# Cumsum-difference matmul on one core: x rows come in another order among the first w blocks, copies are shared anew, and the first five groups get a new order

## The chip, the cores and the metric

The kernel runs on one NeuronCore of a Trainium2 chip. Five engines matter here: TensorE (PE) for matmuls, VectorE (DVE) and ScalarE (ACT) for elementwise work, GpSimd (POOL) for one reduction across partitions, and SyncE (SP), from which all DMA transfers are issued. The metric is the device time of one execution in microseconds; the median of three runs stands for a kernel.

## The reference

```python
def reference(x, w):
    cs = np.cumsum(x, axis=1)
    diff = cs - np.concatenate([np.zeros((cs.shape[0], 1, cs.shape[2])), cs[:, :-1, :]], axis=1)
    return np.matmul(diff, w).astype(np.float32)
```

x is (8, 2048, 2048) and w is (2048, 2048), both float32. The difference of a running sum is x again, so what is computed is x @ w: 16384 rows by 2048 by 2048. The kernel computes that product.

## The kernel before

**Tiling.** x has 128 tiles of 128 rows. The first four tiles ("plain rows") are multiplied in bf16 as they are; the other 124 in f16, in 31 groups of four tiles, by a Strassen-Winograd scheme: seven products of blocks instead of eight, and in most products a second level inside (class `Quarters`: seven quarter products; class `Whole`: eight ordinary half products). The names of the steps are those of the scheme: B11, B21, B12, B22 are scaled f16 blocks of w, T1 to T4 their sums, S1 to S4 sums of x blocks (g and h are the two row pairs of a group), P1 to P5 the five products with a second level, Q1 to Q4 and make1 to make4 the inner sums of w, s1 to s4 the inner sums of x.

**Start.** w comes as 32 blocks `w.h.k` of 128 x 1024 (column half h, row block k), 0.5 MB each. The x rows of the first four tiles come as 16 pieces `first x.q.r` (column quarter q, tile r) of 0.25 MB. DVE casts a pair of pieces (`cast x.q.a`, a = tile pair), PE transposes it through PSUM against an identity built by the `eye` steps (`turn x.q.a`), and DVE or ACT copies it back (`turned x.q.a`). A w block is cast to bf16 (`cast w.h.k`, a ring of seven buffers) and DVE finds its largest magnitude (`max w.h.k`). `plain.h.r.k` are the products of the first four tiles. Before the first of them PE runs dummies (`warm.i`), which read a tile of zeros.

**Scale.** The largest of all maxima goes over the partitions on POOL (`max of all`); from it come `uw` and `uinv`, and with `uinv` the raw w is turned into the blocks (`B11.k` and so on, line 460 on DVE, 462 on ACT). The leftover part of tile 3 (`left over.i`) uses these scaled blocks too. A later row tile t is loaded, weighed (mean magnitude, line 140, ACT), given a scale (line 163, DVE), narrowed to f16 (line 178, ACT) and transposed by DMA (`turn`, line 195).

**Groups.** Period 0 holds the plain rows and the first group, in which nearly all is done at one level. Periods 1 to 30 are one group each: products P1, P2, P5, P3, P4 with 28 matmuls each and 16 half products, 204 matmuls of 512 columns (208 in period 1, whose P1 is a `Whole`). The results leave PSUM by `keep` (a scaled copy, line 624, ACT) and by adds such as `C12g+P3.g` (line 635, DVE); `P.first` and `P.out` (line 627, ACT) copy between PSUM banks or to a chain buffer, `P.middle` and `P.last` (line 576, DVE) add to banks. All matmuls of the groups are lines 588 (half products) and 610 (quarter products).

**Order.** Each step is recorded with a label, an engine and a function; nothing is issued until the end. `emit` then sorts all steps by a key, period number times 1620 plus the label's place in the table `places`, and issues them in that order, each engine's instructions chained so that the order holds. The table has own entries for periods 0, 1, 2, 29, 30 and 31, and one (None) for all others, so period 3 uses the common one. On each engine and on SP's queue the steps run strictly in this order; between engines semaphores make a step wait for what it reads or overwrites. These are the lines that do it:

```python
        for _, _, engine, ask in sorted(ops, key=when) if places else ops:
            after(engine, ask)
```

## Time and profile before

| | before |
|---|---|
| median of 3 runs | 1450.01 us (1449.58 to 1451.32) |
| profiled execution, its span | 1449.2 us |
| PE, DVE, ACT busy | 99%, 92%, 83% of the span |
| granted PE clock, mean | 0.999 |
| DMA | 351.59 MB, mean 243 GB/s |
| first real product (`plain.0.1.0`) | 13.19 us |
| first scaled block of w | 61.04 us |
| first product of periods 2, 3, 4, 5 | 166.09, 210.98, 255.01, 299.04 us |

Times in the profile are microseconds from the span's start. A row of a timeline gives start, duration, engine, line, operation, what it writes and reads (names without buffer numbers), and in brackets how long the engine was idle before it and what ended the wait. A row of a stretch gives for each engine the busy time and the number of instructions. A row of a group gives busy time, mean duration in nanoseconds, and the idle time ahead of its instructions. A busy engine shows overlapping durations: back to back, matmuls of 512 columns start 0.216 us apart though each lasts 0.38.

### The profile page before, as it was taken

How to read it: one execution, taken by the hardware profiler on the slowest of the kernel's cores; microseconds unless marked ns; L12 is line 12 of the kernel's file. 1: busy time of each engine (PE TensorE's matmuls, PEld its weight loads, DVE VectorE, ACT ScalarE, POOL GpSimd, SP SyncE). 2: the span in 40 equal slices, each digit the busy share in tenths (PEclk: the TensorE clock that was granted, in tenths of full speed). 3: DMA queues.
4: the chain of work that ended last, by engine and by line, in shares of the span. 5: the costliest groups of instructions: out<-in, count | busy, mean ns of one | idle time of the engine just before them, and what ended most of it. 6: DMA issues, size and time to landing. Idle time of an engine off the chain costs nothing.

```text
span 1449.2 us, 20358 instructions
## 1 busy us (share of the span) xinstructions
PE 1438.6 (99%) x6692; PEld 652.2 (45%) x6698; DVE 1334.3 (92%) x2345; ACT 1204.5 (83%) x1994; POOL 0.5 (0%) x5
## 2 busy tenths in 40 slices
PE   8999999999999999999999999999999999999998
PEld 4444444444444444444444444444444444444443
DVE  6999999999999999999999999999999999999988
ACT  5997888898888888888988888988888888889783
POOL 0000000000000000000000000000000000000000
PEclk9999999999999999999999999999999999999999
DMA  9999979899888999989998888998989998989973
GB/s 360 369 252 272 252 212 228 240 247 262 226 234 226 243 262 231 244 222 228 247 265 233 228 229 237 252 257 226 222 239 244 260 248 225 218 236 248 264 200 116
DMA packets 343930, 351.59 MB, mean 243 GB/s; under 512 B 270992, under 2 KB 270992, under 8 KB 343824
## 3 DMA queue, kind: packets, MB, share of 16 engines
q1 hardware_dynamic: 343824, 350.29, 89.4%
q8 instruction: 52, 0.85, 0.2%
q14 instruction: 54, 0.44, 0.1%
HBM read 150.99 MB, written 134.22 MB: 197 GB/s over the span
## 4 chain that ended last, share of the span: by engine, by line
PE 91%; issue 4%; DMA 2%; ACT 2%; DVE 1%; DVEq 0%; POOLq 0%; ACTq 0%; SPq 0%
PE b L610 61%; PE b L588 30%; DMA x<-F 1%; DMA F<-in_x_dram 1%; DVE W L460 1%; ACT waste L140 0%; DMA out_dram<-arena 0%; ACT W L462 0%; DVE arena L635 0%; ACT arena L624 0%; ACT F L178 0%; ACT arena L342 0%; ACT arena L178 0%; DVE arena L576 0%; DVE W L576 0%
## 5 line engine op out<-in xcount | busy, mean ns | idle before, releaser
L588 PE MATMUL b<-W,x 128*128 128x512 f16 x2144 | 518.1, 379 | 0.1
L635 DVE SCALAR_TENSOR_TENSOR arena<-b,tiny,arena 128x512 f32<-128x512 f32 x612 | 446.9, 745 | 16.0 <-PE b L610 4.8
L610 PEld LDWEIGHTS <-arena 128*128 128x128 f16 x2744 | 268.2, 98 | 325.4 <-DVE arena L576 6.3
L610 PE MATMUL b<-W,arena 128*128 128x512 f16 x1672 | 413.7, 379 | 0.8 <-DVE arena L576 0.4
L624 ACT ACTIVATE arena<-b,tiny 128x512 f32<-128x512 f32 x496 | 317.0, 684 | 35.4 <-PE b L588 14.9
L588 PEld LDWEIGHTS <-x 128*128 128x128 f16 x2144 | 209.7, 98 | 253.3 <-issue 0.3
L140 ACT ACTIVATE waste<-F,tiny 128x1024 uint8<-128x1024 f32 x246 | 283.9, 1154 | 15.6 <-DMA F<-in_x_dram 14.1
L178 ACT ACTIVATE F<-F,tiny 128x1024 f16<-128x1024 f32 x246 | 282.1, 1147 | 10.9 <-DVE tiny L163 9.4
L610 PE MATMUL b<-W,x 128*128 128x512 f16 x1192 | 287.5, 379 | 0.0
L610 PE MATMUL b<-arena 128*128 128x512 f16 x1072 | 261.6, 379 | 0.0
L610 PEld LDWEIGHTS <-x 128*128 128x128 f16 x1428 | 139.7, 98 | 168.5
L576 DVE TENSOR_TENSOR b<-b,arena 128x512 f32<-128x512 f32 x298 | 205.9, 691 | 5.7 <-ACT arena L627 2.0
L627 ACT COPY b<-b 128x512 f32<-128x512 f32 x149 | 85.5, 574 | 134.4 <-PE b L610 112.4
L627 ACT COPY arena<-b 128x512 f32<-128x512 f32 x298 | 170.2, 580 | 19.9 <-PE b L610 13.0
L576 DVE TENSOR_TENSOR arena<-W 128x2048 f16<-128x2048 f16 (+1 forms) x158 | 185.6, 1176 | 0.4 <-PE b L610 0.4
L576 DVE TENSOR_TENSOR arena<-x,x 128x512 f16<-128x512 f16 (+1 forms) x181 | 91.5, 506 | 50.1 <-PE b L610 50.1
L576 DVE TENSOR_TENSOR x<-x,x 128x1024 f16<-128x1024 f16 x124 | 85.2, 687 | 2.0
L576 DVE TENSOR_TENSOR arena<-W,arena 128x512 f16<-128x512 f16 (+1 forms) x157 | 85.9, 563 | 0.6 <-PE b L610 0.5
L576 DVE TENSOR_TENSOR arena<-arena 128x512 f16<-128x512 f16 x120 | 50.8, 424 | 13.7 <-PE b L610 11.8
L610 PE MATMUL b<-arena,x 128*128 128x512 f16 x236 | 60.3, 379 | 0.0
L324 PE MATMUL b<-arena 128*128 128x512 bf16 x234 | 53.5, 379 | 1.5 <-DVE arena L279 0.8
L576 DVE TENSOR_TENSOR arena<-x,arena 128x512 f16<-128x512 f16 x119 | 49.6, 417 | 0.6 <-PE b L610 0.6
(49 smaller groups left out, 503.6 us busy)
## 6 DMA issues: line engine op xcount, KB each, us to landing
F<-in_x_dram SPq DMA_DIRECT2D x246, 512.0 KB, 5.4
out_dram<-arena SPq DMA_DIRECT2D x240, 512.0 KB, 4.8
W<-in_w_dram SPq DMA_DIRECT2D x31, 512.0 KB, 9.5
out_dram<-arena SPq DMA_DIRECT2D x31, 256.0 KB, 2.7
W<-in_x_dram SPq DMA_DIRECT2D x16, 256.0 KB, 6.6
x<-F SPq DMA_TRANSPOSE x246, 4.4
arena<-in_x_dram SPq DMA_DIRECT2D x2, 512.0 KB, 5.1
W<-in_w_dram SPq DMA_DIRECT2D x2, 256.0 KB, 9.0
```

The costliest lines, as they stand in the source:

```text
L140: lambda: nc.scalar.activation(waste, data, ABS, bias=least, scale=1.0 / ROW, accum_out=m),
L178: lambda: nc.scalar.activation(to, data, COPY, scale=s),
L324: said = nc.tensor.matmul(to[n], xP[:, r, ko, :], b[:, ds(n * NB, NB)], start=(ko == 0), stop=(ko == KO - 1),)
L460: ask = lambda: nc.vector.tensor_scalar(to, src, uinv, None, MUL)
L576: record(label, "dve", lambda: nc.vector.tensor_tensor(dst, p, q, op))
L588: said = nc.tensor.matmul(to[n], a[k], b[k][:, n, :], start=(start and k == 0), stop=(k == KH - 1), skip_group_check=True,)
L610: said = nc.tensor.matmul(to, a[k], b[k], start=(start and k == 0), stop=(k == 3), skip_group_check=True)
L624: record(label, "act", lambda: nc.scalar.activation(c, p, COPY, scale=u))
L627: record(label, "act", lambda: nc.scalar.copy(to, p))
L635: label, "dve", lambda: nc.vector.scalar_tensor_tensor(c, p, u, c, MUL, ADD)
```

## The change

Nothing is added to or removed from the computation except six dummies. Four things change.

- `WARM` falls from 30 to 24. Before, 22 dummies ran ahead of the first transpose, seven between the first and second, one more after it; in the new order 22, one and one.
- `on_two` gives each copy in two forms, for ACT and for DVE, and `record` swaps the engine of the labels in `moved`. Period 0: seven w casts (w.0.0, 0.1, 0.4, 0.7, 0.11, 1.1, 1.14), `turned x.3.1` and `B22.5` go from ACT to DVE; `cast x.2.1`, `out.0.1.0`, `out.0.2.0` and `B22.6` from DVE to ACT. Period 2: two narrows, three keeps and `P4.first` from ACT to DVE. Period 3: one narrow, three keeps and `P5.out4` from ACT to DVE.
- `places` has new orders for periods 0, 1 and 2 and an own one for period 3. On SP's queue w.0.0 comes after six x pieces instead of eight, w.0.2 and w.0.1 before the last two pieces of the second quarter; `load1.0` comes ahead of `turn0.0`. On DVE the zeros that the dummies read come after the first eye rows, and the last two eye rows after casts of x. On PE all leftover products come before the first group's.
- `plainly` and `made` replace `all_seven` and `more`: a table says which product is taken as `Whole`, and which inner sums have been made. With the table as it stands (P1 of period 1 alone) the same products and sums are issued as before.

```diff
-    WARM = 30
+    WARM = 24
...
+    moved = {
+        0: (
+            "cast w.0.0", "cast w.0.1", "cast w.0.4", "cast x.2.1", "cast w.0.7",
+            "turned x.3.1", "cast w.0.11", "cast w.1.1", "out.0.1.0", "out.0.2.0",
+            "cast w.1.14", "B22.5", "B22.6",
+        ),
+        2: (
+            "narrow4.1", "keep C12h.1", "narrow6.1", "P4.first", "keep C21g.0", "keep C21g.1",
+        ),
+        3: (
+            "narrow4.1", "keep C12g.0", "P5.out4", "keep C21g.1", "keep C21h.1",
+        ),
+    }
+
     def record(label, engine, ask):
...
+        if isinstance(ask, dict):
+            if label in moved.get(period[0], ()):
+                engine = {"act": "dve", "dve": "act"}[engine]
+            ask = ask[engine]
         ops.append((period[0], label, engine, ask))
+
+    def on_two(to, src, scale=None):
+        if scale is None:
+            return {
+                "act": lambda: nc.scalar.copy(to, src),
+                "dve": lambda: nc.vector.tensor_copy(to, src),
+            }
+        return {
+            "act": lambda: nc.scalar.activation(to, src, COPY, scale=scale),
+            "dve": lambda: nc.vector.tensor_scalar(to, src, scale, None, MUL),
+        }
+
...
-        record(
-            f"narrow{role(t)}.{i}",
-            "act",
-            lambda: nc.scalar.activation(to, data, COPY, scale=s),
-        )
+        record(f"narrow{role(t)}.{i}", "act", on_two(to, data, s))
...
     places = {
         0: {
-            'first x.0.2': 0, 'first x.1.1': 1, 'first x.0.0': 2, 'first x.1.3': 3,
-            'first x.0.3': 4, 'first x.0.1': 5, 'first x.1.2': 6, 'first x.1.0': 7, 'w.0.0': 8,
-            'zeros': 9, 'least': 10, 'ones': 11, 'numbers': 12, 'numbers turned': 13, 'eye': 14,
-            'eye#2': 15, 'eye#3': 16, 'eye#4': 17, 'cast x.0.1': 18, 'cast w.0.0': 19, 'warm.0': 20,
-            'warm.1': 21, 'warm.2': 22, 'warm.3': 23, 'warm.4': 24, 'warm.5': 25, 'warm.6': 26,
-            'warm.7': 27, 'warm.8': 28, 'warm.9': 29, 'warm.10': 30, 'warm.11': 31, 'warm.12': 32,
-            'warm.13': 33, 'warm.14': 34, 'warm.15': 35, 'warm.16': 36, 'warm.17': 37,
-            'warm.18': 38, 'warm.19': 39, 'warm.20': 40, 'warm.21': 41, 'turn x.0.1': 42,
-            'warm.22': 43, 'warm.23': 44, 'warm.24': 45, 'warm.25': 46, 'warm.26': 47,
-            'warm.27': 48, 'warm.28': 49, 'turned x.0.1': 50, 'cast x.1.0': 51, 'cast x.0.0': 52,
...
+            'ones': 1, 'first x.0.0': 1, 'least': 2, 'first x.0.2': 2, 'numbers': 3,
+            'first x.0.3': 3, 'numbers turned': 4, 'first x.1.1': 4, 'eye': 5, 'first x.0.1': 5,
+            'zeros': 6, 'first x.1.0': 6, 'eye#2': 7, 'warm.0': 7, 'w.0.0': 7, 'warm.1': 8,
+            'w.0.2': 8, 'cast x.0.1': 8, 'warm.2': 9, 'w.0.1': 9, 'eye#3': 9, 'cast w.0.2': 9,
+            'warm.3': 10, 'first x.1.3': 10, 'cast x.0.0': 10, 'warm.4': 11, 'w.0.3': 11,
+            'eye#4': 11, 'warm.5': 12, 'first x.1.2': 12, 'cast x.1.0': 12, 'warm.6': 13,
+            'w.0.4': 13, 'cast w.0.0': 13, 'warm.7': 14, 'w.0.5': 14, 'warm.8': 15,
+            'first x.2.0': 15, 'warm.9': 16, 'first x.2.2': 16, 'warm.10': 17, 'first x.2.1': 17,
+            'warm.11': 18, 'w.0.6': 18, 'warm.12': 19, 'w.0.7': 19, 'warm.13': 20,
+            'first x.2.3': 20, 'warm.14': 21, 'w.0.8': 21, 'warm.15': 22, 'first x.3.0': 22,
+            'warm.16': 23, 'w.0.9': 23, 'warm.17': 24, 'first x.3.1': 24, 'warm.18': 25,
+            'w.0.10': 25, 'warm.19': 26, 'first x.3.2': 26, 'warm.20': 27, 'first x.3.3': 27,
+            'warm.21': 28, 'w.0.11': 28, 'turn x.0.1': 29, 'w.0.12': 29, 'warm.22': 30,
+            'w.0.13': 30, 'turn x.0.0': 31, 'w.0.14': 31, 'warm.23': 32, 'w.0.15': 32,
+            'turned x.0.0': 33, 'w.1.0': 33, 'turned x.0.1': 34, 'plain.0.1.0': 34,
+            'plain.0.0.0': 35, 'cast w.0.1': 35, 'plain.0.2.0': 36, 'max w.0.2': 36,
...
+            'plain.0.3.11': 89, 'w.1.3': 89, 'turned x.3.1': 89, 'plain.0.0.11': 90,
+            'max w.0.11': 90, 'w.1.6': 90, 'plain.0.2.11': 91, 'max w.0.12': 91, 'w.1.15.0': 91,
+            'plain.0.1.11': 92, 'max w.0.14': 92, 'w.1.5': 92, 'plain.0.1.12': 93, 'max w.0.13': 93,
+            'w.1.11': 93, 'plain.0.3.12': 94, 'max w.1.0': 94, 'w.1.7': 94, 'plain.0.2.12': 95,
+            'cast w.1.1': 95, 'w.1.9': 95, 'plain.0.0.12': 96, 'max w.0.15': 96, 'w.1.8': 96,
+            'plain.0.2.13': 97, 'max w.1.4': 97, 'w.1.10': 97, 'plain.0.1.13': 98, 'max w.1.2': 98,
...
+            'plain.1.1.7': 139, 'plain.1.2.7': 140, 'plain.1.1.8': 141, 'cast w.1.14': 141,
...
+            'weigh0.0': 149, 'plain.1.3.9': 150, 'weigh0.1': 150, 'plain.1.1.10': 151, 'mean0': 151,
+            'plain.1.1.11': 152, 'unit0': 152, 'scale0': 152, 'plain.1.0.12': 153, 'B22.0': 153,
+            'B11.2': 153, 'plain.1.1.12': 154, 'B11.6': 154, 'weigh2.0': 154, 'plain.1.0.13': 155,
+            'B11.7': 155, 'narrow0.0': 155, 'plain.1.0.14': 156, 'B11.3': 156, 'narrow0.1': 156,
+            'plain.1.3.10': 157, 'B11.5': 157, 'weigh2.1': 157, 'plain.1.0.15': 158, 'B21.2': 158,
+            'plain.1.2.10': 159, 'load1.0': 159, 'B21.7': 159, 'plain.1.3.11': 160, 'turn0.0': 160,
+            'B21.0': 160, 'plain.1.3.12': 161, 'turn0.1': 161, 'B21.3': 161, 'plain.1.3.13': 162,
+            'B21.5': 162, 'plain.1.1.13': 163, 'B21.4': 163, 'plain.1.2.11': 164,
...
+            'left over.0': 173, 'out.1.3.1': 173, 'left over.1': 174, 'mean2': 174,
+            'out.1.0.0': 175, 'scale2': 175, 'left over.2': 175, 'B11.0': 176, 'weigh1.0': 176,
+            'left over.3': 176, 'T1.3': 177, 'A11g B11.0.0': 177, 'narrow2.0': 177, 'B11.4': 178,
+            'A12g B21.1.0': 178, 'out.1.3.0': 178, 'turn2.0': 178, 'T1.6': 179, 'A11g B11.0.1': 179,
...
         1: {
+            'weigh4.1': -1329, 'P1h.1.1': -1329, 'S3g': -1328, 'P5.0': -1328, 'keep C11h.0': -1328,
+            'P2.6': -1327, 'keep C11h.1': -1327, 'P5.s1': -1326, 'C11g+P2.g.1': -1325, 'S2g': -1324,
+            'put0.0': -1324, 'in1.make1.1': -1323, 'S2g T2.0.0': -1323, 'P5.1': -1322,
+            'P5.s2': -1321, 'P2.last': -1320, 'C11h+P2.h.0': -1319, 'S3h': -1318, 'P5.first': -1318,
+            'in5.make4.0': -1317, 'weigh6.0': -1317, 'P5.2': -1317, 'S2h': -1316,
+            'S2g T2.0.1': -1316, 'mean4': -1316, 'C11h+P2.h.1': -1315, 'P5.out2': -1315,
...
         2: {
+            'P3.3': -2826, 'P3.out2': -2826, 'P3.s3': -2825, 'weigh5.0': -2825, 'in3.Q3': -2824,
+            'P3.s4': -2823, 'P3.4': -2823, 'P3.middle': -2822, 'turn4.1': -2822,
+            'C12g+P3.g.0': -2821, 'P3.5': -2821, 'P3.out4': -2821, 'in4.Q1': -2820,
...
+            'mean5': -2819, 'C12h+P3.h.0': -2818, 'P4.1': -2818, 'put0.1': -2818, 'scale5': -2817,
...
+        3: {
+            'P1.0': -4420, 'P1.1': -4419, 'P2.0': -4418, 'P1.first': -4416, 'P2.1': -4415,
...
+            'keep C21h.1': 2559, 'put3.1': 2559, 'P2.s2': 2560, 'load8.1': 2560,
```

More of the change, by code (lines that the diff above doesn't have):

```diff
@@ L335, with result @@
     results_at = iter(results * 2)
-    def result(name, p, rows, columns, u=None):
+    def result(name, p, rows, columns):
         c = next(results_at)
-        if u is None and name in ("out.0.1.0", "out.0.2.0"):
-            record(f"{name}", "dve", lambda: nc.vector.tensor_copy(c, p))
-        elif u is None:
-            record(f"{name}", "act", lambda: nc.scalar.copy(c, p))
-        else:
-            record(f"{name}", "act", lambda: nc.scalar.activation(c, p, COPY, scale=u))
+        record(name, "dve" if name in ("out.0.1.0", "out.0.2.0") else "act", on_two(c, p))
         done.append(
@@ L815, in slot, with plainly, made @@
                 matmuls(*halves_of(f"{self.name}{name}", to, a, self.right, True)[at % 4])
+    def plainly(name, g):
+        return name in {PLAIN + 4: ('P1',)}.get(g, ())
+    making = {}
+    def made(name, inner, how):
+        if name not in making:
+            making[name] = True
+            how(inner)
     def group_plain(g):
@@ L972, in group @@
         P1.slot(1)
-        if more:
+        if not P1.plain:
             in_1.give("Q4")
@@ L1015, in group @@
         P1.slot(6)
-        if not more:
-            make_5(in_5)
-        in_5.give("Q3")
+        if not P5.plain:
+            made("P5", in_5, make_5)
+            in_5.give("Q3")
         C11h = keep("keep C11h", Y, uh, free.pop(1))
@@ L1033, in group @@
         total("S4g", S4g, A12g, S2g, SUB)
-        if not more:
-            make_1(in_1)
+        if not plainly("P1", g + 4):
+            made("P1", in_1, make_1)
+        if not plainly("P2", g + 4):
+            made("P2", in_2, make_2)
         go(2)
@@ L1162, in group @@
         P4.slot(6)
+        if P4.plain and not plainly("P4", g + 4):
+            made("P4", in_4, make_3)
+        if P5.plain and not plainly("P5", g + 4):
+            made("P5", in_5, make_5)
+        if P3.plain and not plainly("P3", g + 4):
+            made("P3", in_3, make_3)
         turn(next_l, [1])
```

69 lines of the change are left out of this document (38 added, 31 removed), and 454 rows, old and new, of the table places.

## The prediction

> **What bounds the kernel now.** I read the page's first part, then the table by stretches of time, then the timelines where that table shows idle time.
>
> ```profile
> PE 1438.6 (99%) x6692; PEld 652.2 (45%) x6698; DVE 1334.3 (92%) x2345; ACT 1204.5 (83%) x1994; POOL 0.5 (0%) x5
> ```
>
> TensorE (PE) is busy for 99% of the span, so little can be won. Where it isn't busy is seen by stretches; the cuts are the first real product (13.19), the scale of w (61.04), and the first product of each group from the second on.
>
> ```profile
> core 0: us, PE busy (x) PEld busy (x) DVE busy (x) ACT busy (x) POOL busy (x), PEclk, DMA share, GB/s
> 13.19:33.34 20.15, 19.88 (x111) 9.77 (x115) 14.05 (x14) 15.57 (x17) 0.00 (x0) 1.00 1.03 404
> 33.34:61.04 27.70, 27.26 (x131) 12.56 (x132) 26.82 (x28) 24.35 (x29) 0.35 (x1) 1.00 1.03 407
> 61.04:117.43 56.39, 56.04 (x258) 25.06 (x258) 55.73 (x97) 50.79 (x79) 0.00 (x0) 1.00 1.00 266
> 117.43:166.09 48.66, 47.82 (x221) 21.45 (x220) 47.05 (x103) 37.73 (x63) 0.00 (x0) 1.00 0.96 236
> 166.09:210.98 44.89, 44.89 (x209) 20.30 (x208) 43.05 (x78) 38.41 (x65) 0.00 (x0) 1.00 0.85 234
> 210.98:255.01 44.03, 44.03 (x205) 19.94 (x204) 40.93 (x73) 38.35 (x65) 0.00 (x0) 1.00 0.93 247
> 255.01:299.04 44.03, 44.03 (x205) 19.94 (x204) 40.75 (x73) 37.48 (x64) 0.00 (x0) 1.00 0.87 236
> ```
>
> From 166 us on TensorE has no idle time at all; periods 3 and 4 take 44.03 us each, and the orders from period 4 on are not touched. What can move is what lies before 166 us: the 13.19 us ahead of the first real product, and PE idle of 0.27, 0.44, 0.35 and 0.84 us in the four stretches behind it. VectorE (DVE) is nearly full there too: idle 0.88, 0.66, 1.61, 1.84 and 3.10 us in the stretches from 33.34 to 255.01. DMA is full until 61 us (share 1.03, 404 to 407 GB/s). So there are three bounds in a row: DMA, then DVE and PE together, then PE alone.
>
> The profiled execution spans 1449.2 us; the median of three runs is 1450.0, 0.8 more. I sum differences and set them against the median. What this measurement can tell from no change is about 0.2%, 2.9 us.
>
> **Start: earlier, and worth nothing.**
>
> ```profile
> 0.00:14.00 14.00, 10.31 (x57) 4.88 (x59) 7.04 (x16) 3.71 (x4) 0.19 (x4) 1.00 0.83 291
> 1.17 6.24 PE L362 MATMUL b<-arena 128*128 128x512 bf16 x22 [1.17 <-DVE arena L237]
> 9.09 0.62 PE L269 MATMUL b<-waste,W 128*128 128x128 bf16 x8 [1.68 <-DVE W L260]
> 8.34 0.69 DVE L260 CAST W<-W 128x1024 bf16<-128x1024 f32 x1 [5.08 <-DMA W<-in_x_dram]
> 11.57 1.05 ACT L313 CAST arena<-W 128x1024 bf16<-128x1024 f32 x1 [9.57 <-DMA W<-in_w_dram]
> 13.19 1.04 PE L324 MATMUL b<-arena 128*128 128x512 bf16 x3 [0.79 <-DVE arena L279]
> 33.43 7.17 DVE L305 TENSOR_REDUCE tiny<-W 128x1 f32<-128x1024 f32 x6 [0.35 <-DMA W<-in_w_dram]
> ```
>
> Today w.0.0 is the ninth transfer on SP's queue and lands at 11.57. The new order puts it seventh, two x pieces of 0.26 MB sooner: 0.52 MB at 404 GB/s is 1.3 us, so about 10.3. Its cast moves from ACT (1.05) to DVE (0.69), and "turned x.0.0" queues behind it on DVE for another 0.69: first product at about 11.7, 1.5 us sooner. "zeros" comes later on DVE, so the dummies begin about 1.2 us later; 22 of them still take 6.24 us and end by about 8.7, ahead of the second x cast and the last "eye" rows that the transposes wait for (their x lands as late as today). The six dummies left out stood in waiting time: 0.
>
> None of the 1.5 us survives. At 33.43 DVE, idle, waits for w.0.12 itself, and PE has been fed block by block until then (idle 0.27 us in 20.15). All 16 x pieces and w.0.0 to w.0.10 stand ahead of w.0.11 in both orders, and the bytes are the same. An earlier start only puts waits between 12 and 33 us. Value 0; ends -1.5 (if kept) and +0.5 (a cast on DVE stuck behind a reduction).
>
> **From w.0.11 to the scale of w.** B11 and B21 need the largest |w|, so the last reduction counts.
>
> ```profile
> 56.69 2.96 ACT L313 CAST arena<-W 128x1024 bf16<-128x1024 f32 x3 [0.31 <-DMA W<-in_w_dram]
> 49.06 10.81 DVE L305 TENSOR_REDUCE tiny<-W 128x1 f32<-128x1024 f32 x10
> 60.58 0.15 DVE L453 TENSOR_SCALAR tiny<-tiny 128x1 f32<-128x1 f32 x1 [0.48 <-POOL tiny L451]
> 61.04 2.74 DVE L460 TENSOR_SCALAR W<-W,tiny 128x1024 f16<-128x1024 f32 x4
> ```
>
> Nine whole reductions and a half one in 10.81 us: 1.13 each, 0.6 for the half. At 56.69 ACT waits for w.1.13; one block of 0.52 MB at 407 GB/s later, at about 58.0, w.1.14 is there, yet DVE's last reduction ends at 59.9: DVE is behind by 0.8. In the new order DVE has, from w.0.11's landing (one block before 33.4, so 32.1): its cast, 0.69, then 21 whole reductions (23.7), two halves (1.2), "turned x.3.1" and "cast w.1.1" (0.65 each, in place of the two copies out.0.1.0 and out.0.2.0 that go to ACT), in all to about 59.0, and w.1.14's own landing plus 1.13 allows 59.1. So 0.8 sooner. "cast w.1.14" now lies in the 0.48 us in which DVE waits for POOL; 0.1 of it sticks out. The scaled blocks begin at 60.3 instead of 61.04: **-0.7**, ends -0.9 and 0.
>
> **Blocks and first products.**
>
> ```profile
> 70.15 2.75 PE L588 MATMUL b<-W,x 128*128 128x512 f16 x12
> 75.33 10.52 PE L588 MATMUL b<-W,x 128*128 128x512 f16 x48
> L460 DVE TENSOR_SCALAR W<-W,tiny 128x1024 f16<-128x1024 f32 x18 | 12.2, 748 | 0.1
> ```
>
> Four blocks in 2.74 us (the last shows its full 0.75) are 0.66 apart. Today B22.7 is among them and the leftovers are strewn between products; at 75.33 all 11 leftover matmuls and the 16 of "A11g B11" are done. The new order makes 15 blocks in a row before the first T1, 9.9 us, with two tiny scales to 70.4; PE does all leftovers first and begins A11g at about 70.6. 16 matmuls at 0.216 (48 in 10.52) bring it to the same point at 74.1: 1.3 sooner, of which 0.7 was counted. **-0.6** more, ends -0.8 and 0.
>
> This needs row 4 transposed by 70.6. The new order puts load1.0 ahead of turn0 on SP's queue.
>
> ```profile
> 65.06 1.34 SPq L195 DMA_TRANSPOSE x<-F  x1
> 66.51 0.99 SPq L517 DMA_DIRECT2D arena<-in_x_dram  x2
> x<-F SPq DMA_TRANSPOSE x246, 4.4
> ```
>
> Issue stays near 65.5 (it hangs on load0's landing, ACT's weighing and narrowing); 4.4 us to landing gives 69.9, margin 0.7. 0; ends 0 and +1.3 (one more block of 0.52 MB ahead of it).
>
> **Waits in periods 0 and 1.** The second fence groups DVE's instructions from 61 to 255 us by form (mean in ns); back to back they start 0.08 us closer than they last.
>
> ```profile
> 86.10 3.63 PE L588 MATMUL b<-W,arena 128*128 128x512 f16 x16 [0.25 <-DVE arena L576]
> 136.99 1.02 PE L610 MATMUL b<-W,arena 128*128 128x512 f16 x4 [0.40 <-ACT b L627]
> 138.45 1.90 PE L610 MATMUL b<-W,arena 128*128 128x512 f16 x8 [0.44 <-DVE arena L576]
> 135.53 0.75 DVE L635 SCALAR_TENSOR_TENSOR arena<-b,tiny,arena 128x512 f32<-128x512 f32 x1 [0.41 <-ACT arena L624]
> ```
> ```profile
> L635 DVE SCALAR_TENSOR_TENSOR arena<-b,tiny,arena 128x512 f32<-128x512 f32 x69 | 49.7, 742 | 0.9 <-ACT arena L624 0.4 <-PE b L610 0.3
> L543 DVE SCALAR_TENSOR_TENSOR W<-W,tiny 128x1024 f16<-128x1024 f32 x8 | 9.9, 1276 | 0.0
> L576 DVE TENSOR_TENSOR W<-W 128x512 f16<-128x512 f16 x44 | 17.2, 417 | 0.1
> L576 DVE TENSOR_TENSOR x<-x,x 128x1024 f16<-128x1024 f16 x16 | 11.0, 685 | 0.2
> L576 DVE TENSOR_TENSOR arena<-W 128x2048 f16<-128x2048 f16 x15 | 18.3, 1217 | 0.2 <-PE b L610 0.2
> ```
>
> These three waits make up most of the 0.35 + 0.84 us of idle PE in the third and fourth stretches. The first is S1g: in the new DVE order eight T1 (9.5), a block, "out" and two C11g adds (0.66 each), one T2 and S1g (0.6 each), one make1 (0.33) and a scale follow on 70.4: S1g ends near 84.2, and PE arrives at 74.1 + 48 x 0.216 = 84.4. The other two come from "C11h+P2.h.0", which waits for ACT's "keep C11h.0" and holds up P5.first. The new order keeps C11h directly behind C11g, ahead of weigh6 and mean4, and puts two units of PE work between P5.0 and P5.1. **-1.2**, ends -1.5 and 0.
>
> **Eleven copies more on DVE in periods 2 and 3.**
>
> ```profile
> L340 DVE COPY arena<-b 128x512 f32<-128x512 f32 x2 | 1.4, 680 | 0.0
> L178 ACT ACTIVATE F<-F,tiny 128x1024 f16<-128x1024 f32 x37 | 42.5, 1148 | 4.2 <-DVE tiny L163 3.7
> L624 ACT ACTIVATE arena<-b,tiny 128x512 f32<-128x512 f32 x64 | 41.3, 683 | 7.4 <-DMA out_dram<-arena 3.6 <-PE b L588 3.2 <-PE b L610 0.4
> 237.95 0.42 DVE L576 TENSOR_TENSOR arena<-x,x 128x512 f16<-128x512 f16 x1 [1.88 <-PE b L610]
> ```
>
> Three narrows leave ACT (1.15 each) for DVE at a block's price, 0.66; eight copies out of PSUM (0.68 on ACT) for DVE at about 0.6 to 0.68, as L340: 2.0 + 4.9 = 6.9 us. ACT is idle 6.5 and 5.7 us in those periods, so its relief brings nothing. DVE's idle time from 61 to 255 is 7.2 us; PE coming 2.5 us earlier (0.7 + 0.6 + 1.2) takes 2.5 off. DVE begins 0.7 earlier, and the new order lets "C22h+Y.1", "keep C21h.1" and P2.s2, 1.6 us, slip behind the first product of period 4. 7.2 - 2.5 + 0.7 + 1.6 = 7.0 against 6.9: it fits only if DVE never waits. It will; 1.88 us of today's idle time is one wait for PE. Both orders added up show where: from the first block to P3.middle of period 2 DVE has 102 short sums (0.33), 63 of 0.6 to 0.65, 39 scaled adds (0.66), 20 blocks and narrows (0.66), 8 T1, 9 wide sums (1.13), 14 scales and one keep, in all 133 us, and ends at 193.6; PE, 142 units of 0.863 after 70.6, wants it at 193.2. So DVE is late by 0.4 there, and as the result is only there 0.1 to 0.2 after the next start, by some 0.6; the same for P3.4 (in3.Q3) and P4.1 (C12g+P3.g.1). I take **+0.7**, ends 0 and +4.9 (all idle time of periods 2 and 3 stays, 1.84 + 3.10). The other moves (B22.5 against B22.6, cast x.2.1) swap equals: 0.
>
> **Sum:** -0.7 - 0.6 - 1.2 + 0.7 = -1.8: **1448.2 us**, 0.12% down.
>
> **A cold clock.** Today's 22 dummies take 6.24 us, and at 0.216 apart they would take 4.9: a start of PE from rest costs 1.3. The granted clock reads 1.00 throughout, so it is the row that shows it. In the new order only two dummies, not eight, stand between the first transpose and the first product. If PE slowed down again there, it would cost at most 1.3 once more, at 12 to 16 us, where the 1.5 us that w.0.12 takes back would cover it: the sum stays at -1.8, and without that cover it is -0.5. [...]
>
> **Rivals.**
> 1. *Full gain.* DVE is never late and the waits before 61 us (0.27 + 0.44) go in part as well: -2.5 - 0.5, 1447.0. For it: every cut is where a wait stands today. Against: DVE's balance of 0.1 us.
> 2. *No gain.* w.1.14 lands where it does, and DVE meets its casts or blocks late by a reduction (1.13) or so in 32 to 60 us; P5 and period 2 get new waits for those removed: 1450.0. For it: DVE idle of 0.88 us in 27.70.
> 3. *Slower.* DVE cannot shed its waits in periods 2 and 3, so the 6.9 us come on top: +4.9 and up to 6.9 against -2.5, about 1453.5. It costs more than it brings from 2.5 us of kept idle time, and is slower by over 0.2% from 5.4. Against: DVE also waits less when PE waits.
> 4. *turn0 late*: +1.3, 1449.5.
> 5. *A second cold start, uncovered*: +1.3, 1449.5. Against: today PE idles 1.68 us before 9.09, and the stretch behind 13.19 shows 0.27 us of idle PE.
>
> **How the numbers follow.** Forecast (1447.2 to 1449.3) 0.42, full gain 0.22, no gain 0.17, slower 0.14, turn0 0.03, clock 0.02. Faster by over 0.2% is below 1447.1: rival 1, 0.22. Slower is rival 3, 0.14. The rest 0.64. The range 1446.8 to 1452.2 takes in the forecast, rivals 2, 4 and 5 and nearly all of 1, and leaves out most of 3. The likeliest case alone: 1447.2 to 1449.3.
>
> **What would show it.** First product near 11.7, yet w.0.12's reduction still near 33.4; blocks begin at 60.2 to 60.5; "A11g B11" at 70.5 to 70.8; period 2's first product about 2.5 us sooner with one unit more of period 1 behind it (near 162.7); period 4's near 253.2, then 44.03 a period; DVE idle in periods 2 and 3 down to some 2 us. I am wrong if blocks begin after 60.8, if A11g waits for a transpose, or if PE idles over 2 us between 166 and 255.

## The result: 9 us slower, made in four periods

| | before | after |
|---|---|---|
| median | 1450.25 us (1449.58 to 1451.32) | 1459.48 us (1459.07 to 1460.81) |
| ratio, 95% interval | | 1.0065 (1.0053 to 1.0078) |
| span of the profiled execution | 1449.2 us | 1457.9 us |
| first product of periods 1, 2 | 117.43, 166.09 us | 113.02, 165.81 us |
| first product of periods 3, 4, 5 | 210.98, 255.01, 299.04 us | 214.22, 262.55, 307.40 us |

(Period 1's first product comes earlier among the products of period 0 in the new order, and one unit of 0.86 us of period 1 now lies behind period 2's first product; so only the later marks compare directly.) From period 5 on the kernels need 44.03 and 44.05 us a period. Nearly all is lost before.

The page's first part and the stretches of the changed kernel, cut at the same events as before (first real product, 61.04, first product of periods 1 to 5; the cut of period 3 lies one matmul behind its first):

```profile
PE 1439.6 (99%) x6686; PEld 651.3 (45%) x6692; DVE 1342.7 (92%) x2361; ACT 1190.9 (82%) x1978; POOL 0.9 (0%) x5
```
```profile
12.75:33.34 20.59, 20.22 (x120) 10.18 (x124) 17.29 (x20) 13.63 (x14) 0.00 (x0) 1.00 1.04 404
33.34:61.04 27.70, 27.59 (x134) 12.82 (x135) 27.35 (x30) 23.29 (x28) 0.71 (x1) 1.00 1.03 407
61.04:113.03 51.99, 51.94 (x241) 23.38 (x241) 50.74 (x85) 48.19 (x77) 0.00 (x0) 1.00 1.07 272
113.03:165.81 52.78, 50.57 (x234) 22.55 (x233) 49.89 (x111) 40.31 (x67) 0.00 (x0) 1.00 0.88 232
165.81:214.44 48.63, 46.69 (x215) 20.67 (x214) 46.77 (x84) 34.19 (x60) 0.00 (x0) 1.00 0.84 233
214.44:262.55 48.11, 44.70 (x205) 19.59 (x204) 43.20 (x77) 33.50 (x56) 0.00 (x0) 1.00 0.80 207
262.55:307.40 44.85, 44.43 (x206) 19.80 (x205) 42.05 (x76) 37.50 (x65) 0.00 (x0) 1.00 0.91 237
```

PE's idle time is a row's length less its busy time. Up to 113 us it is now smaller than before (0.37 + 0.11 + 0.05 us) and the first product comes 0.44 us sooner: the start and the blocks did win about 1 us. Then come 2.21, 1.94, 3.41 and 0.42 us of idle PE where before had 0.84 and three times nothing. VectorE's idle time in periods 2 and 3 rose too, from 4.94 to 6.77 us (1.86 + 4.91), although it has eleven copies more to do. More work alone does not explain that. ScalarE, which was relieved, has at most 34.2 us of work in 48. So the engines wait for one another. The next two views say for what: ScalarE's weighs between 61 and 262 us, before (first fence) and after (second), and VectorE's instructions that read PSUM, after, from 61 to 255 us (before's first row stands in the prediction: 0.9 us idle, 0.4 of it for ACT).

```profile
L140 ACT ACTIVATE waste<-F,tiny 128x1024 uint8<-128x1024 f32 x37 | 42.5, 1148 | 4.3 <-DMA F<-in_x_dram 4.1
```
```profile
L169 ACT ACTIVATE waste<-F,tiny 128x1024 uint8<-128x1024 f32 x36 | 41.3, 1148 | 13.7 <-DMA F<-in_x_dram 13.6
```
```profile
L650 DVE SCALAR_TENSOR_TENSOR arena<-b,tiny,arena 128x512 f32<-128x512 f32 x64 | 46.7, 746 | 3.9 <-ACT arena L147 3.8
L148 DVE TENSOR_SCALAR arena<-b,tiny 128x512 f32<-128x512 f32 x4 | 3.0, 750 | 2.4 <-ACT arena L147 2.2 <-PE b L603 0.3
```

ScalarE stands in front of a weigh (line 169) for 13.6 us until its load has landed, where it stood 4.1; and VectorE waits 6.0 us for ScalarE's copies (line 147), where it waited 0.4. The chain of waits around the worst place, period 3's first products, puts the two together (start, duration, what; the row "issue" is time in which nothing shown was waited for):

```profile
208.52 4.23 DMA F<-in_x_dram
...
213.11 1.25 ACT waste L169 x2
...
214.58 1.26 ACT arena L147 x2
215.84 0.03 issue
215.86 0.03 DVE arena L650
215.90 0.63 issue
216.53 0.41 DVE arena L591
216.95 1.32 DVE arena L650 x2
```

`load7.1`, issued 3.8 us later than in the kernel before (at 208.52 instead of 204.76), lands at 212.75, `weigh7.1` runs, and only then, because they stand behind it on ScalarE, the two C21h copies. VectorE's "C22h+Y.1" (line 650) starts 0.03 us after the second copy ends, with 2.17 us of idle time ahead of it (timeline, the same place):

```profile
215.86 0.75 DVE L650 SCALAR_TENSOR_TENSOR arena<-b,tiny,arena 128x512 f32<-128x512 f32 x1 [2.17 <-ACT arena L147]
...
218.32 1.02 PE L625 MATMUL b<-arena 128*128 128x512 f16 x4 [1.35 <-DVE arena L650]
```

It needs nothing that the copy writes. Both read the same PSUM bank, and in the trace VectorE's, the later of the two in the program, is released by the end of the copy. (In f1_bank below VectorE's stands first in the program: there it is the last of four adds back to back from 210.80 to 213.52 us, and the two copies begin at 213.83.) At all five long waits of this kind (0.95, 0.60, 2.17, 1.56 and 1.47 us, at 164.6, 196.0, 215.9, 237.8 and 261.2 us) the copy and VectorE's instruction read one bank. Behind the first four PE waits too (1.17, 0.57, 1.35 and 1.68 us, over at 168.0, 198.3, 218.3 and 239.2 us); behind the fifth it waits 0.1 and 0.3 us. Why the two reads here wait for each other the traces do not show. One of the five comes from an order that the change turned round ("C22g+X.1" in period 1), two from copies that went to VectorE while the other reader of their bank stayed on ScalarE ("keep C12h.1", "keep C12g.0"); the last two stand as before, but behind a later ScalarE.

### The profile page after: what moved, and what is told of

Read it like the earlier page. It is cut to its first block, busy times and chain, and to the rows that moved or that the text cites. A ratio compares the mean times of both kernels' runs of the same rounds, so it can differ in the third digit from the quotient of the medians.

```text
span 1457.9 us, 20349 instructions
## 1 busy us (share of the span) xinstructions
PE 1439.6 (99%) x6686; PEld 651.3 (45%) x6692; DVE 1342.7 (92%) x2361; ACT 1190.9 (82%) x1978; POOL 0.9 (0%) x5
## 4 chain that ended last, share of the span: by engine, by line
PE 89%; DVE 4%; DMA 3%; ACT 2%; issue 1%; SPq 0%; DVEq 0%; ACTq 0%
PE b L625 57%; PE b L603 29%; PE b L348 3%; DVE arena L650 2%; DVE arena L591 1%; DMA W<-in_x_dram 1%; DMA F<-in_x_dram 1%; DMA x<-F 1%; ACT arena L147 1%; DVE b L591 1%; ACT waste L169 1%; DMA out_dram<-arena 0%; DVE W L591 0%; ACT F L147 0%; PE b L491 0%
## 5 line engine op out<-in xcount | busy, mean ns | idle before, releaser
L650 DVE SCALAR_TENSOR_TENSOR arena<-b,tiny,arena 128x512 f32<-128x512 f32 x612 | 447.8, 746 | 20.3 <-ACT arena L147 6.9
L147 ACT ACTIVATE arena<-b,tiny 128x512 f32<-128x512 f32 x490 | 313.2, 683 | 33.2 <-PE b L603 16.2
L169 ACT ACTIVATE waste<-F,tiny 128x1024 uint8<-128x1024 f32 x246 | 283.9, 1154 | 24.5 <-DMA F<-in_x_dram 23.2
L147 ACT ACTIVATE F<-F,tiny 128x1024 f16<-128x1024 f32 x243 | 278.6, 1147 | 13.1 <-DVE tiny L192 11.9
L143 ACT COPY arena<-b 128x512 f32<-128x512 f32 (+1 forms) x317 | 182.7, 588 | 31.0 <-PE b L625 19.3
```

The costliest lines, as they stand in the source:

```text
L143: "act": lambda: nc.scalar.copy(to, src),
L147: "act": lambda: nc.scalar.activation(to, src, COPY, scale=scale),
L169: lambda: nc.scalar.activation(waste, data, ABS, bias=least, scale=1.0 / ROW, accum_out=m),
L650: label, "dve", lambda: nc.vector.scalar_tensor_tensor(c, p, u, c, MUL, ADD)
```

## The experiments

The theory **order**: the new tables put copies behind waits in in-order queues, and the shared banks carry these waits to VectorE and PE. The rival **load** (the prediction's third): VectorE cannot take 6.9 us more, wherever it stands. (Line numbers of the kernels below differ by some lines: L147, L151 and L166 are the same scaled copy, L650, L654 and L669 the same add, L169, L173 and L188 the weigh.)

Idle PE by stretch in the profiled executions, us (a stretch's length less PE's busy time; the stretches end at each kernel's own first product of periods 1 to 5), and the length from period 2's first product to period 5's:

| kernel | median | first product | to 61 | to period 1 | period 1 | 2 | 3 | 4 | length 2 to 4 |
|---|---|---|---|---|---|---|---|---|---|
| before | 1450.25 | 13.19 | 0.71 | 0.35 | 0.84 | 0 | 0 | 0 | 132.95 |
| after | 1459.48 | 12.75 | 0.47 | 0.05 | 2.21 | 1.94 | 3.41 | 0.42 | 141.59 |
| e1_orders_only | not read | 12.90 | 0.45 | 0.36 | 2.05 | 5.41 | 2.47 | 1.19 | 146.16 |
| e2_moves_only | 1454.57 | 13.22 | 0.64 | 0.48 | 0 | 2.13 | 0.90 | 0.16 | 137.73 |
| e3_new01 | not read | 12.51 | 0.54 | 0.29 | 3.20 | 0 | 0 | 0 | 133.04 |
| e4_new23 | not read | 12.77 | 0.73 | 0.31 | 0 | 2.39 | 3.27 | 0.41 | 140.85 |
| f1_bank | 1456.62 | 12.31 | 0.17 | 0.14 | 1.30 | 2.17 | 2.05 | 0.33 | 140.31 |
| f6_weighs | 1462.33 | 12.61 | 0.23 | 0 | 1.76 | 0.89 | 3.76 | 0.40 | 143.71 |
| f7_all | 1460.27 | 13.41 | 0 | 0 | 4.77 | 0.47 | 1.19 | 0.33 | 137.42 |
| g2_turn5 | 1460.92 | 12.99 | 0 | 0 | 2.81 | 2.27 | 3.74 | 0.84 | 144.11 |
| g1_all | 1457.57 | 13.08 | 0.11 | 0.73 | 2.66 | 0.42 | 0.67 | 0.32 | 136.86 |
| g3_start | 1450.76 | 12.82 | 0.21 | 0.43 | 0.37 | 0 | 0 | 0 | 133.30 |
| h1_new0 | 1452.20 | 12.42 | 0.25 | 2.29 | 0 | 0 | 0 | 0 | 132.95 |
| h2_new01 | 1452.33 | 12.54 | 0.28 | 0 | 2.54 | 0.18 | 0 | 0 | 133.78 |

(The last column contains 0.86 us more work where the new order of period 2's first product holds. A slow clock, told of below, lengthens PE's busy time, not its idle time: in f6_weighs, at a granted 0.50, nine matmuls make PE busy for 3.49 of the 3.50 us from 238.0 on. And a wait costs an estimated 0.16 us more than the idle time shown: the matmul ahead of it lasts 0.38 us, where back to back the next one starts after 0.216.)

**Order and copies apart.**

```diff
     moved = {
         0: (
...
-        2: (
...
-        3: (
...
     }
```

> The changed kernel with its whole new order, but the eleven copies of periods 2 and 3 back on ScalarE. Theory 'load' (VectorE cannot take 6.9 us more): the loss behind period 2's first product goes, and only what period 1 lost stays: about 1453. Theory 'order' (the new order puts copies behind waits in ScalarE's and SP's queues, and a VectorE instruction that reads the same bank as a ScalarE copy waits for that copy): the PE gaps at 166 (1.3 us) and 216 (1.5 us) stay, and only the two that hang on a copy moved to VectorE (0.7 us at 197, 1.8 us at 237) go: 1456 to 1458.

> The kernel before with its own order, and only the eleven copies of periods 2 and 3 moved to VectorE. Theory 'load': VectorE's idle time in those periods (1.84 + 3.10 us) stays and 6.9 us come on top, 4 to 5 us slower: about 1455. Theory 'order': in the order of before the copy of the other tile of the same bank stands ahead on ScalarE seldom, the 4.9 us of idle time take most of the copies, 1 to 2 us slower: about 1451.5.

In the first the last three periods were given the common order in place of their own, which changes what these periods compute and what they cost, so its end says nothing; it is read at period 28's first product: 1325.4 us, against 1311.7 before and 1320.5 after. So with the copies back on ScalarE the new order is not better but 4.9 us worse than the changed kernel (one profiled execution each). An estimated 1.7 us of that is the clock, granted at 0.58 from 218.4 to 222.0 us and at 0.99 from there to 236. Neither theory had that. Its rows at period 3's start (timelines of ScalarE, then of PE) show why: ScalarE waits twice for loads, four copies stand behind them in a row, and PE waits 2.97 us.

```profile
211.34 1.15 ACT L173 ACTIVATE waste<-F,tiny 128x1024 uint8<-128x1024 f32 x1 [1.77 <-DMA F<-in_x_dram]
...
214.24 1.15 ACT L173 ACTIVATE waste<-F,tiny 128x1024 uint8<-128x1024 f32 x1 [1.65 <-DMA F<-in_x_dram]
...
215.71 2.40 ACT L151 ACTIVATE arena<-b,tiny 128x512 f32<-128x512 f32 x4
```
```profile
218.45 1.38 PE L629 MATMUL b<-W,x 128*128 128x512 f16 x4 [2.97 <-DVE arena L654]
```

The second (the order of before, eleven copies moved, no other edit) is 4.2 us slower: ratio 1.0030 (1.0019 to 1.0042). That is what **load** said, and too much for **order**. Its stretches of periods 2 and 3 show a VectorE that is nearly full:

```profile
164.79:212.55 47.76, 45.63 (x209) 20.05 (x208) 45.62 (x82) 33.98 (x59) 0.00 (x0) 1.00 0.83 218
212.55:258.10 45.55, 44.65 (x206) 19.64 (x205) 43.81 (x78) 35.46 (x60) 0.00 (x0) 1.00 0.91 234
```

These periods took 88.9 us before, with 84.0 us of work for VectorE; 89.4 us of work would not fit into them even if VectorE never waited. Its idle time fell only from 4.94 to 3.88 us. So both causes are real, and they are not a sum: the moved copies cost 4.2 us in the old order and save 4.9 us in the new one, which needs them because ScalarE stands so long.

**Which periods.** The spliced kernels take all steps ahead of a named one from one order and all others from the other:

```python
early = [s for s in new_order if new_rank[s] < new_rank[2, "P1.0"]]
order = early + [s for s in old_order if s not in early]
```

> The new order (and its engines) up to period 2's first product, the order of before behind it, copies of periods 2 and 3 on ScalarE. Both theories: the lead of 1.5 us at 78 us and the loss of about 2 us in period 1 (a gap of 1.7 us at 136) stay as in the changed kernel, and the 8.8 us behind it go: 1450.0 to 1451.5. If it comes out over 1453, the loss of periods 2 and 3 was carried over from period 1.

> The order of before up to period 2's first product, the new order and the moved copies behind it. If the loss belongs to periods 2 and 3 themselves (both theories): 1450 + 8.8 = 1458 to 1459. If it is there because period 1 arrived late with its loads and copies: 1450 to 1453.

> As in the run that left out the last three groups' orders: the new order up to period 2's first product, the order of before behind it, now with those orders. That run was 2.5 us behind the kernel before at group 28's first product and lost nothing from period 2 on: 1452.5 to 1453. If its loss came from the profiled execution alone: 1450.3.

The first two had the same fault in the last three periods and are read at period 28: 1314.3 (2.5 us behind before) and 1317.9 (6.2 behind). The third is the first with its own last orders: 1452.33, ratio 1.0016 (1.0007 to 1.0025), and no idle PE to speak of from period 2 on. So periods 0 and 1 cost 2.4 us of the 9.2, and periods 2 and 3 the other 6.8; the second, in which only these two have the new order, agrees with its 6.2.

**The shared banks.** Every engine keeps its sequence; only the program order between the engines is changed, so that VectorE's reader comes first. Its core (numbers are the places in the tables):

```diff
-'keep C21g.1': -1269, 'keep C21h.1': -1266, 'weigh7.1': -1265,
+'keep C21g.1': -1264.7, 'keep C21h.1': -1264.6, 'weigh7.1': -1264.5,
...
-'C12g+X.0': -2827, 'keep C12h.1': -2826, 'C21g+P4.g.0': -2800, 'C22h+Y.1': -2799,
+'C12g+X.0': -2827.3, 'keep C12h.1': -2827.2, 'C21g+P4.g.0': -2800.3, 'C22h+Y.1': -2800.2,
...
-'P5.middle': -4381, 'keep C12g.0': -4380, 'C22g+X.0': -4344,
+'P5.middle': -4381.3, 'keep C12g.0': -4381.2, 'C22g+X.0': -4344.2,
```

> The changed kernel; every engine's instructions stay in the same sequence. At five places in periods 1 to 3, where a ScalarE copy and a VectorE instruction read the same PSUM bank, VectorE's is put first in the program, so that it no longer waits for ScalarE's copy. Theory 'order' (those waits, 0.95, 0.60, 2.17, 1.56 and 1.47 us of idle VectorE, hold up PE): the PE gaps behind them (1.3 us at 166, 0.7 at 197, 1.5 and 0.7 at 216 to 226, 1.8 at 237, 0.75 at 263) shrink by about 5 us together: about 1454.5. Theory 'load' (VectorE has 6.9 us too much work and would be late anyway): the waits turn up elsewhere, under 1.5 us gained: 1458 to 1459.5.

1456.62, ratio 1.0040 (1.0028 to 1.0053): some 3 us better than the changed kernel, between the two theories. The gap at 216 is gone. But from period 2's first product to period 5's it saves only 1.3 us (140.31 against 141.59); the rest lies in period 1 and at the start, where the edit touches little, and may belong to this one execution. Two of the waits came back at once with another cause, in the same places (its timeline of VectorE, twice):

```profile
166.16 0.75 DVE L669 SCALAR_TENSOR_TENSOR arena<-b,tiny,arena 128x512 f32<-128x512 f32 x1 [1.59 <-ACT arena L166]
```
```profile
235.58 0.75 DVE L167 TENSOR_SCALAR arena<-b,tiny 128x512 f32<-128x512 f32 x1 [1.56 <-DMA out_dram<-arena]
```

The first waits for the next shared copy, behind `weigh7.0`; the second ("keep C12g.0") for a result to leave the buffer that it writes.

**The loads.** First edit: `load8.1` ahead of `turn7` on SP (period 0), `scale5` behind `T4.5` on VectorE (period 0), `narrow5` ahead of `P4.out2` on ScalarE (period 2).

```diff
-'turn7.0': 275, 'load8.1': 278, 'scale5': 246, 'narrow5.0': 247, 'narrow5.1': 248, 'weigh7.0': 249,
+'turn7.0': 276.4, 'load8.1': 276.3, 'scale5': 249.3, 'narrow5.0': 249.4, 'narrow5.1': 249.5, 'weigh7.0': 249.6,
...
-'narrow5.0': -2813, 'narrow5.1': -2808,
+'narrow5.0': -2814.4, 'narrow5.1': -2814.3,
```

> The changed kernel with three waits for a load taken off the queues: in period 0 load8.1 stands ahead of turn7.0 and turn7.1 on SP's queue instead of behind them, and scale5 stands behind T4.5 on VectorE instead of ahead of it; in period 2 ScalarE's narrow5.0 and narrow5.1 stand ahead of P4.out2, so that load7.1's buffer comes free 3.7 us sooner. Theory 'order': the PE gaps at 114.5 (0.86), 136.3 (1.68) and 216 (1.5) go or shrink, weigh4.1 of period 1 begins near 132 instead of 134.8: 3 to 4 us gained, about 1456. Theory 'load': the gap at 136 may go, as no moved copy is near it; that at 216 stays: 1457.5 to 1458.

> Both edits together. Theory 'order': they share only the gap at 216: about 6.5 us gained, 1453, with under 3 us of PE gaps left from 113 us on. Theory 'load': at most 3 us, 1456.5 or more.

1462.13 and 1457.72. These two change what is computed: `narrow5.1` of period 0 now stands behind `load7.1`, which takes over its buffer, so that it narrows other rows, and waits for them, which puts a new gap of 2.5 us at 120 to 123. They say nothing for or against the first part of their expectation; of the rest, the gap at 216 shrank only in the second, where the banks were turned round as well.

**The weighs.** ScalarE's order alone, at three places, to what the kernel before has:

```diff
-'weigh4.1': -1329, 'weigh7.0': -1270,
+'weigh4.1': -1317.5, 'weigh7.0': -1265.5,
...
-'weigh7.0': -2807, 'weigh7.1': -2806, 'mean7': -2805, 'keep C21h.1': -2800,
+'weigh7.0': -2799.5, 'weigh7.1': -2799.4, 'mean7': -2799.3, 'keep C21h.1': -2801.1,
```

> The changed kernel with ScalarE's order alone changed at three places, to what the kernel before has there: in period 1 weigh4.1 stands behind the two C11h copies and P5.first, and weigh7.0 behind keep C21g.1 and keep C21h.1; in period 2 weigh7.0, weigh7.1 and mean7 stand behind the C21h copies, the second half first. Theory 'order' (a weigh waits for its load, and the copies that PE and VectorE want stand behind it): the PE gaps at 136 (1.7 us), 166 (1.3) and 216 to 226 (2.2) go or shrink to under half: about 1455. Theory 'load' (VectorE's moved copies): the gap at 136 goes, the others stay: 1457.5 to 1458.

1462.33, 2.9 us worse than the changed kernel, and a miss for both. The gaps at 166 and 216 shrank as **order** said (period 2: 0.89 us of idle PE instead of 1.94). But PE then reached period 3's shared copy some 2.5 us earlier, while that copy still stood behind `weigh6` and its load (its timelines of VectorE and PE, and two stretches):

```profile
236.61 0.75 DVE L167 TENSOR_SCALAR arena<-b,tiny 128x512 f32<-128x512 f32 x1 [2.87 <-ACT arena L166]
```
```profile
238.01 1.44 PE L644 MATMUL b<-W,arena 128*128 128x512 f16 x3 [2.99 <-DVE arena L163]
```
```profile
234.00:238.00 4.00, 1.02 (x5) 0.39 (x4) 1.39 (x4) 3.97 (x9) 0.00 (x0) 0.90 0.36 143
238.00:241.50 3.50, 3.49 (x9) 1.26 (x9) 3.50 (x7) 1.36 (x3) 0.00 (x0) 0.50 0.00 0
```

The gap grew to 3 us, and behind it the clock was granted at 0.50 from 238.0 to 241.5 us and at 0.94 on average from there to 264.28, which is an estimated 6 us at 0.50, up to 244.0. That half clock, an estimated 3 us by these figures, is what makes the run slower than the changed kernel: PE's idle time in periods 2 to 4 is less, 5.05 us instead of 5.77, and yet they take 2.1 us more. (All five executions have a mean granted clock of 0.998, those of the changed kernel 0.999.) So what was taken off the gaps at 166 and 216 was worth nothing here, as the next load-bound place had no slack.

**All repairs together,** `weighs`, `banks`, `narrow5` and `load8.1` as above without the edit of `scale5`:

> The same, with VectorE's instruction first at the banks that both engines read, load8.1 of period 0 ahead of turn7.0 on SP's queue, and narrow5.0 and narrow5.1 of period 2 ahead of P4.out2 on ScalarE. Theory 'order': PE's idle time from 113 us to 307 us falls from 10.2 us to about 4, as in that stretch only the gaps at 114.5, 237 and a few of 0.3 us are left: about 1453. Theory 'load': VectorE is busy for 90 of the 89 us that PE needs for periods 2 and 3, so over 3 us of gaps stay in these two alone, wherever they stand: 1455 to 1456.

1460.27. In periods 2 to 4 it does what **order** said: idle PE 1.99 instead of 5.77 us, 4.2 us shorter. In period 1 it loses more than that: `weigh4.1` behind P5.first and `load8.1` ahead of `turn7` made VectorE's S1h wait for the transposed rows, and PE stands for 4.3 us up to 140.0, with the clock at 0.50 behind it from 139.8 to 144.0 (0.97 from 130 to 139.8 and 0.94 from 144 to 160: an estimated 139.2 to 145.9). Then period 1 by SP's queue, first by itself, then with the repairs but with `weigh4.1` where it was:

```diff
-'put3.1': 264, 'load8.0': 265, 'turn5.1': 266, 'turn5.0': 267, 'turn7.0': 275, 'load8.1': 278,
+'turn5.0': 263.5, 'turn5.1': 263.6, 'put3.1': 264, 'load8.0': 265, 'load8.1': 274.6, 'turn7.0': 275,
```

> The changed kernel; only SP's queue in period 0 is changed: turn5.0 and turn5.1 stand ahead of put3.1 and load8.0 instead of behind them, and load8.1 ahead of turn7.0. Theory 'order' (load8.1 waits for turn5 to land and free its buffer, turn5 stands behind put3.1, which waits for its sum; weigh4.1 waits for load8.1, and the C11h copies and P5.first behind it on ScalarE hold up PE): load8.1 is issued near 125 instead of 129.6, and the gap of 1.7 us at 136 goes: about 1457.8. If the period's loss is VectorE's: the gap moves on to P5.3 or P3, 1459 to 1459.5.

> The same edit of SP's queue, together with those that took 4.4 us of idle PE out of periods 2 to 4 before (VectorE first at the shared banks, weigh7 behind the C21 copies, narrow5 of period 2 ahead of P4.out2), and weigh4.1 where the changed kernel has it. Theory 'order': PE's idle time from 113 us on falls from 10.4 to 4 to 5 us: 1453 to 1454.5. Theory 'load': what is taken off one place comes back within the same periods: 1456 or more.

The first: 1460.92 (1459.09 to 1463.32), no gain. `load8.1` is issued at 124.9 as meant, but lands at 131.7, and `turn7.1` lands 2 us later than in the changed kernel, so that S1h waits for it (2.57 us of idle VectorE, over at 133.47): the DMA was full there already in the changed kernel (share 1.05 from 118 to 140 us), and what one transfer won another lost. The second: 1457.57, ratio 1.0049 (1.0037 to 1.0062), with these stretches for periods 2 to 4:

```profile
169.13:215.97 46.84, 46.42 (x213) 20.53 (x212) 45.81 (x82) 33.20 (x58) 0.00 (x0) 1.00 0.91 242
215.97:261.44 45.47, 44.80 (x206) 19.86 (x205) 43.49 (x78) 35.74 (x61) 0.00 (x0) 1.00 0.89 223
261.44:305.99 44.55, 44.23 (x205) 19.68 (x203) 41.74 (x75) 37.58 (x65) 0.00 (x0) 1.00 0.92 237
```

1.41 us of idle PE instead of 5.77, 136.86 us instead of 141.59: the queue repairs take back 4.7 of the 7.8 us by which these three periods had grown (0.86 of the 7.8 is the unit that changed sides). What is left is about 3.1 us, 2.5 of it in periods 2 and 3 with a VectorE busy for 89.3 of their 92.3 us. That fits **load**; it was not taken apart further. The median is worse than these periods say, as this kernel still loses in period 1 and in its start (below).

**The start.** Only the start, in three cuts: up to the first product with T1, up to the block B11.0 (which is the fifteenth of the blocks in the new order, not the first, as the expectation has it), and up to the first block, the last with B22.5 and B22.6 on the engines of before.

> The new order, the moved casts and the 24 dummies up to the first product with T1 (85 us in the changed kernel), the order of before behind it, all copies behind it on the engines of before. If the start and the blocks bring what the changed kernel showed at 61 us (first product 0.44 us sooner, 0.8 us less idle PE behind it) and the old order keeps it: 1449.0. If the lead of the start is lost wherever the next wait for a load stands: 1450.0 to 1450.5.

> The new order, the moved casts and the 24 dummies up to the first scaled block of B11 alone (61 us), the order of before behind it, copies behind it on the engines of before. If the start's lead of 1.2 us (first product 0.44 sooner, 0.8 us less idle PE) is kept: 1449.0. If the order of before has it back by period 1, or waits for blocks that come in another order: 1450 or more.

> The new order, the moved casts and the 24 dummies up to the first scaled block (60 us), the order of before behind it, with B22.5 and B22.6 on the engines of before as well. If the start's lead (0.4 us at the first product, 0.8 us less idle PE up to 61 us) is kept behind it: 1449.0. If it is worth nothing, as the prediction had it: 1450.3. If the blocks are what needs the new start or hinder it, as in the two starts tried: 1452 or more, with the wait at a product of S1g or S2g.

1457.00, 1458.38 and 1450.76. The first two keep B22.6 on ScalarE, but in the old order's place, behind two weighs; VectorE stands 5.65 us for it (timeline of the second):

```profile
97.90 1.29 DVE L595 TENSOR_TENSOR W<-W 128x1024 f16<-128x1024 f16 x2 [5.65 <-ACT W L151]
```

So they price that move out of place, not the start. The third is the start alone: ratio 1.0003 (0.9994 to 1.0012), worth nothing that can be measured. And period 0 as a whole, with the order of before behind it:

> The new order and its engines up to period 1's first product (113 us in the changed kernel), the order of before behind it, the copies of periods 2 and 3 on ScalarE. If period 1's loss is made by period 1's own new order, this keeps the little that the start brings and loses nothing behind it: 1449.5 to 1450.5. If period 0's new order hands over its sums, loads and copies in a state that period 1 pays for whatever its order: idle PE of 1.5 to 3 us between 113 and 166 us, 1451.5 to 1453.

1452.20, ratio 1.0015 (1.0006 to 1.0024): nothing is lost in period 1, but 2.29 us at the seam ahead of it, most of it in one wait of PE for a copy that stands behind `narrow5` on ScalarE, which waits for VectorE's late `scale5` (its timelines of ScalarE and PE):

```profile
116.12 2.33 ACT L151 ACTIVATE F<-F,tiny 128x1024 f16<-128x1024 f32 x2 [3.69 <-DVE tiny L196]
```
```profile
119.08 1.02 PE L607 MATMUL b<-W,x 128*128 128x512 f16 x4 [1.80 <-ACT arena L151]
```

But this wait belongs to the splice: `scale5` runs at 115.94 us here, at 113.82 in the kernel before and at 112.48 in the changed one. So the run doesn't price period 0's order, and for periods 0 and 1 together h2_new01's 2.4 us stand. Its longest wait of PE, 1.25 us up to 137.7, corresponds to the changed kernel's 1.51 us up to 138.2: P5.first stands on ScalarE behind `weigh4.1` and its load, and `load8.1` is issued at 129.59 us in the changed kernel, at 124.87 before. Which step of the new order makes that load late was not separated. No version tried beats the kernel before.

## Why the prediction was wrong

**What bounds the kernel: right, and not used to the end.** What could be won was the first product's time and PE's waits up to 166 us, by the table shown 1.90 us of idle time. The prediction then booked 0.7 + 0.6 + 1.2 = 2.5 us of gains behind the first product. The idle time is no strict limit, as each wait costs an estimated 0.16 us more than it shows (0.38 less 0.216), but nearly every wait would have had to go; the sum should have been held against it.

**Start, 0: right in size.** The first product came at 12.75, not 11.7: w.0.0 landed at 11.37, not at 10.3, and PE waited 1.65 us for its cast on VectorE. VectorE no longer waits for w.0.12 (its reduction begins at 35.9), so the reason given was not the one; but the start alone measured 1.0003.

**Blocks, -0.7 and -0.6: half.** They begin at 60.63 instead of 60.3, and A11g at 71.43 instead of 70.6. PE ran without a gap up to there: what it could win was its idle time, 1.06 us up to period 1, and it won half of that. `turn0` landed in time (70.6 and 71.5), so rival 4 did not come.

**Periods 0 and 1, -1.2: wrong.** The two waits at 137 to 138 belong to the profiled execution. The two other kernels with the order of before up to there have no idle PE in period 1 at all. And that execution does not stand for the median: times here are some 1.8 us above the spans, so a span of 1449.2 is a time of about 1451, 1 us too long; the prediction had taken it for 0.8 too short. And the new order brought its own waits there, 2.21 us.

**Periods 2 and 3, +0.7 (ends 0 and +4.9): the step that failed.** It balanced VectorE's time, 7.0 us of idle against 6.9 of copies, and counted ScalarE's relief as nothing because ScalarE idles. Measured: 6.8 us, beyond its upper end. Two things were missing. VectorE's idle time is tied to waits and could hardly be filled (the copies alone cost 4.2 us in the old order and took 1.1 of its 4.94 us; the "against" of rival 3, that VectorE waits less when PE waits, did not hold). And the new order itself was read for VectorE and PE alone: on ScalarE `weigh7` had moved ahead of the C21 copies, and at three banks the two readers had changed order or engine. Neither was in the sum, nor in the upper end, which took idle time as something that can stay but not grow.

**Rivals.** The third, slower, had the sign and half of the mechanism; at 1453.5 it was 6 us short for the same reason. The fifth, the second cold start, came in four of the fifteen executions with the new start (below), but not in the changed kernel's. Of the marks named for being wrong, "PE idles over 2 us between 166 and 255" came true, with 5.35 us up to 263.

## What to carry to other kernels

Where engines run in fixed orders, a balance of busy time is only a lower bound: read each queue for the instructions that wait for a transfer, and for what stands behind them. When copies change engine or place, look at who else reads their PSUM bank: here the reader that comes later in the program stood behind the queue of the earlier one, for 2.17 us at 215.9. And hold the sum of gains against the bottleneck's idle time, from more than one execution.

## What was not expected of the hardware

Behind some waits of PE of 1.99 us and more the clock was granted at 0.50 to 0.64 again, at the start and in the middle of the kernel. After the last dummy the new start waits for w.0.0's cast. In four of the fifteen profiled executions with the new start that wait was 1.99 to 2.98 us and the granted clock in 13.5 to 17 us was 0.52 to 0.64; in the others it was at most 1.89 us and the clock 1.00. The first six products, in the timelines of f7_all and of the changed kernel:

```profile
13.41 2.74 PE L367 MATMUL b<-arena 128*128 128x512 bf16 x6 [2.98 <-DVE arena L163]
```
```profile
12.75 1.47 PE L348 MATMUL b<-arena 128*128 128x512 bf16 x6 [1.65 <-DVE arena L144]
```

0.43 us apart instead of 0.216, so 1.3 us lost on these six alone. The length of the wait alone did not decide it: in the middle, one of 2.06 us (g2_turn5, at 218.8) was followed by eight products in 3.57 us at a clock of 0.54 (220.6 to 224.1), one of 2.47 us (f3_both) by fourteen in 3.18 us at 1.00 (119.0 to 125.5; timelines of PE):

```profile
220.83 3.57 PE L644 MATMUL b<-arena 128*128 128x512 f16 x8 [2.06 <-DVE arena L669]
```
```profile
122.15 3.18 PE L622 MATMUL b<-W,x 128*128 128x512 f16 x14 [2.47 <-ACT arena L166]
```

What else decided it the runs do not show. In these kernels a wait of nearly 3 us with a slow clock behind it cost half as much again at the start of f7_all (2.98 us of waiting, then 0.60 on average from 13.5 to 17 us, an estimated 1.4 us), and as much again in f6_weighs (2.99 us, then the estimated 3 us).
